# Scans of a gated DeltaNet block: projections beside them in parts of six products, and sums of squares with 128 columns of weights

## The chip, the cores and the metric

The kernel runs on one core of a Trainium2 chip. TensorE (PE) multiplies matrices into PSUM; VectorE (DVE), ScalarE (ACT) and GpSimd (POOL) do the elementwise work; SyncE (SP) issues most of the transfers. The metric is the time of one execution on the device in microseconds. A measurement is the median of several runs.

## What is computed

One block of a streaming encoder for a sequence of 1024 frames with 1024 channels in float32: half a SwiGLU layer, a mixing layer with two groups of heads (a gated spatial unit, and 4 heads of a gated delta rule), another half SwiGLU layer, and a last norm. The change touches only the delta rule. Cut to that:

```python
qkv = jax.nn.silu(causal_dwconv(qkv, dn_conv_w[l])).astype(jnp.float32)
q, k, v = jnp.split(qkv, 3, axis=-1)
q = l2norm(q.reshape(B, T, DN_HEADS, DN_HEAD_DIM))
k = l2norm(k.reshape(B, T, DN_HEADS, DN_HEAD_DIM))
...
sol = lax.linalg.triangular_solve(L + eye, rhs, left_side=True, lower=True, unit_diagonal=True)
u_c, w_c = sol[..., :Dv], sol[..., Dv:]
...
def step(S, inp):
    qd, kd, uc, wc, a, gl = inp
    v_new = uc - jnp.einsum('bhcd,bhde->bhce', wc, S)
    o = jnp.einsum('bhcd,bhde->bhce', qd, S) + jnp.einsum('bhij,bhje->bhie', a, v_new)
    S = S * jnp.exp(gl)[..., None, None] + jnp.einsum('bhcd,bhce->bhde', kd, v_new)
    return S, o
```

The recurrence over chunks (`step`) is the scan: each state `S` needs the one before it.

## The kernel before

The two SwiGLU layers take most of the time (`ffn`). Between them stands `middle`, where the delta rule is worked out in eight halves: 4 heads, each with two halves of the sequence of 512 frames. A half (class `Half`) holds four tiles of 128 frames and goes through these methods, all written as generators that yield between steps:

- `inverse`: five steps that put the inverse of a triangular matrix together from blocks of 32 and 64 rows, and its product with the keys. Each step is one group of small fp32 matmuls into a bank of `ps_a` (tag `ax`, two banks), and a copy or a subtraction out of it by ACT or DVE, into a buffer of the tag `rv` or into `Z` and `X`.
- `values`: two steps, transposes of the values (`VT`) and the product with `Z`, which give `u`.
- `queries`: two steps. The first squares the queries on ACT and sums them over channels by matmuls with a column of ones; the second makes the products of keys and queries.
- `scan`: for each of the four tiles two products with the state (`sc` and `sq`), a subtraction from `u` on DVE, a yield, the product `sd` that updates the state, and a yield. After the eighth yield comes a closing part: the product of `aT` and `u` (`ax<-u,aT` in the profile), its sum of squares on ACT, a norm, and multiplications with the gate `zt` and the norm on POOL. `zt` is loaded at the start of the scan into a buffer of the tag `rv`, of which there are two.

While a scan runs, its stage also issues the filler. `proj_steps` is one: the projection of one block of 128 channels of queries or values for the whole sequence. For each half of the sequence it makes 8 steps over the contraction, each of three products of 128x128 by 128x512 (`mm3`: high by high, high by low, low by high, since a float32 number is held as a rounded part of type fp32r and the rest), all into one bank of `ps_m`; then a copy to `pad` on ACT, a convolution of one multiplication (L1000) and three multiply-adds (L1002) on DVE, and a SiLU on ACT. Before the change it yields after each step of three products. The other filler is the preparation of later halves: nine small steps. In the stage of a first half `x` of head h these are `y.values`, `y.queries` and `nx.inverse` (`first`), in that of a second half `ny.inverse`, `nx.values` and `nx.queries` (`second`), where `y` is the second half of the same head and `nx`, `ny` are the halves of the next.

`weave(few, many, gaps)` mixes the two by hand: for each number n in `gaps` it issues n parts of the projection and then one small step. `stage(x, filler, rate)` runs the scan and pulls `rate` steps of the filler after each of its yields, and what is left once the scan's closing part is written. `beside` adds a step of the spatial unit's mixing (`mixing`) at the second, fifth and eighth small step. The framework orders instructions by this order of writing, but puts an instruction that is ready ahead of an earlier one that is not, by its own estimate of times, when it compiles; on the chip each engine runs its instructions in that order.

The stages that the change touches are five: the first halves of heads 0, 1 and 2 (projection of the next head's queries) and the second halves of heads 0 and 1 (projection of the values of the head after next). The second half of head 2 and both halves of head 3 have another filler, `token_steps` of the gated spatial unit (`u0`, `u1`), which is not changed.

Of the kernel before, what the change touches and what calls it, by code (L numbers as in the profile page):

```python
# [17 lines left out]
P = 128  # L18
T = 1024
D = 1024  # L20
KC = 8
NCH = 22
HEADS = 4
# [7 lines left out]
def block_kernel(ctx: ExitStack, tc, a, out):  # L31
# [579 lines left out]
    with ExitStack() as mid:  # L611
        ps_a, ps_s, ps_m = psums(mid, (2, 1, 3))
        tl = pool(mid, "tl")
        up = pool(mid, "up")
        lv = pool(mid, "lv")
        ep = pool(mid, "ep")
        ts = pool(mid, "ts")
        kp = pool(mid, "kp")
        wp = pool(mid, "wp")
        yblk = middle(tc, nc, a, locals())  # L620
# [190 lines left out]
def middle(tc, nc, a, L):  # L811
# [4 lines left out]
    bank, mm, mm3, split, rpow, rsqrt = L["bank"], L["mm"], L["mm3"], L["split"], L["rpow"], L["rsqrt"]  # L816
# [49 lines left out]
    def steps(name, ch, ev, **kw):  # L866
        w = a[f"w{name}"][ch]
        return token_steps([w[0], w[1]], 256, ev, hT, **kw)
# [6 lines left out]
    def sc(name, n=32):  # L875
        return ts.tile([P, n], F32, tag=name, name=name)
# [70 lines left out]
    def v4(t):  # L947
        return t.rearrange("p (t n) -> p t n", t=4)
# [4 lines left out]
    def tl(t):  # L953
        return slice(t * P, (t + 1) * P)

    def big(name, bufs=1):
        p = {"VT": lv, "rv": lv, "aT": lv, "u": up}.get(name, late)
        return p.tile([P, 512], F32, tag=name, name=name, bufs=bufs)
# [4 lines left out]
    def four(lf, rf, pp=(ps_a, "ax"), w=P):  # L963
        ps = bank(*pp)
        for t in range(4):
            mm(ps[:, t * w:t * w + w], lf(t), rf(t), start=True, stop=True)
        return ps
# [7 lines left out]
    def load_qkv(blk, behind=None):  # L975
        with tc.issue_after(behind.ins) if behind else nullcontext():
            return load_w(a["wqkv"][blk]).rearrange("p s (k n) -> p s k n", k=KC)

    def proj_conv(blk, dsts):
        for _ in proj_steps(blk, load_qkv(blk), dsts):  # L980
            pass

    def proj_steps(blk, w, dsts):
        prev = None
        for half in range(2):
            h = hT[half]
            ps = bank(ps_m, "mm")
            for k in range(KC):
                mm3(ps, w[:, 0, k], w[:, 1, k], h[k // 4][:, 0, k % 4], h[k // 4][:, 1, k % 4], k == 0, k == KC - 1)
                if k < KC - 1:  # L990
                    yield
            pad = ts.tile([P, 528], F32, tag="pad", name="pad", bufs=2)
            if half == 0:
                nc.gpsimd.memset(pad[:, 0:3], 0.0)
            else:
                nc.gpsimd.tensor_copy(pad[:, 0:3], prev[:, 512:515])
            prev = pad
            nc.scalar.copy(pad[:, 3:515], ps)
            acc = ep.tile([P, 512], F32, tag="acc", name="acc", bufs=2)
            nc.vector.tensor_scalar(acc, pad[:, 0:512], cw[:, blk, 0:1], None, op0=ALU.mult)  # L1000
            for j in range(1, 4):
                nc.vector.scalar_tensor_tensor(acc, pad[:, j:j + 512], cw[:, blk, j:j + 1], acc, op0=ALU.mult, op1=ALU.add)  # L1002
            d = dsts[half]
            nc.scalar.activation(d, acc if len(d.shape) == 2 else v4(acc), AF.Silu)
            yield

    def inv_norm(ss, scale, add, name):
        r = small("r" + name)
        nc.vector.tensor_scalar(r, ss, scale, add, op0=ALU.mult, op1=ALU.add)
        rpow(r, r, 4)  # L1010
        return r
# [48 lines left out]
    class Half:  # L1060
# [66 lines left out]
        def queries(self):  # L1127
            q = self.wq[:, :, P:256]
            aT = self.aT = big("aT", 2)
            nc.scalar.activation(v4(aT), q, AF.Square)  # L1130
            ssq = bank(ps_a, "ax")[:, :4]
            for t in range(4):
                for c in (0, 64):
                    mm(ssq[c:c + 64, t:t + 1], aT[:, t * P + c:t * P + c + 64], ones, start=True, stop=True)
            self.rq = inv_norm(ssq, P, P * EPS, "q")
            yield
            aps = four(lambda t: self.ks[:, 0, tl(t)], lambda t: q[:, t])
            nc.vector.tensor_tensor(aT, aps, EA[self.h][:, self.hf], op=ALU.mult)
            yield
# [39 lines left out]
    ones = sc("ones", 128)[:, 0:1]  # L1179
# [82 lines left out]
    def load_ya():  # L1262
        y = xp.tile([P, 2, 512], F32, tag="x", name="ya")
        t = 2 * len(ya)
        nc.sync.dma_start(y, sp["m"][t:t + 2].rearrange("t p n -> p t n"))
        ya.append(y)
# [24 lines left out]
    def values_of(h):  # L1291
        for x in H[h]:
            x.VT = big("VT", 4)
        return [x.VT for x in H[h]]

    def new_wq(x):
        x.wq = xp.tile([P, 4, 256], F32, tag="x", name="wq")

    def queries_of(h):
        return [x.wq[:, :, P:256] for x in H[h]]  # L1300


    def weave(few, many, gaps):
        for n in gaps:
            yield from islice(many, n)
            yield from islice(few, 1)
        yield from many
        yield from few
# [4 lines left out]
    def beside(steps):  # L1313
        for i, s in enumerate(steps):
            if i in (1, 4, 7):
                next(mixed, None)
            yield s

    def stage(x, filler, rate):
        due = 0.0  # L1320
        for _ in x.scan():
            due += rate
            while due >= 1:
                due -= 1
                next(filler, None)
        for _ in filler:
            pass
# [3 lines left out]
    with tc.issue_after(solved.ins):  # L1331
        wv, wq_ = load_qkv(9), load_qkv(1)
        together(proj_steps(8, w8, values_of(0)))
        together(proj_steps(0, w0, queries_of(0)))
# [4 lines left out]
    for h in range(HEADS):  # L1339
        x, y = H[h]  # L1340
        if h + 1 < HEADS:
            nx, ny = H[h + 1]
            nx.load()

            def first():
                yield from y.values()
                yield from y.queries()
                yield from nx.inverse()

            def queries():  # L1350
                for z in (nx, ny):
                    new_wq(z)
                yield from proj_steps(h + 1, wq_, queries_of(h + 1))

            def second():
                yield from ny.inverse()
                yield from nx.values()
                yield from nx.queries()

            if h + 2 < HEADS:  # L1360
                wv = load_qkv(10 + h, solved)
            else:
                u0 = steps("u", 0, ev_u0, part=2)
            stage(x, weave(beside(first()), queries(), (1,) + (2,) * 8), 2)
            ny.load()
            if h + 2 < HEADS:
                wq_ = load_qkv(h + 2)
                more = proj_steps(10 + h, wv, values_of(h + 2))
            else:
                more = islice(u0, 16)  # L1370
            stage(y, weave(beside(second()), more, (1, 1, 2, 2, 2, 2, 2, 2, 2)), 2)
        else:
            stage(x, weave(chain(y.values(), y.queries()), islice(u0, 8), (0, 1, 1, 1, 0)), 1.5)
            stage(y, u0, 1)
            u1 = steps("u", 1, ev_u1, part=2, tiles=(0, 4, 1, 5, 2, 6, 3, 7))
            for _ in range(4):
                load_ya()
            together(u1)
# [75 lines left out]
```

## Time and profile before

| what | value |
|---|---|
| three runs | 1818.42, 1818.73, 1819.32 us; median 1818.73 |
| the profiled execution | 1816.45 us |
| its span | 1814.4 us |
| mean granted clock of TensorE | 0.994 |
| instructions | 24818 |
| first scan's first product (`sc`) | at 867.6 us |
| last scan's closing product (`ax<-u,aT`) | at 1035.9 us |
| sums of squares (`ax<-ones,aT`) | 128 matmuls, 128 weight loads |

The page gives each engine's busy time, and the span in 40 slices, so that a stage can be found. The scans lie between about 867 and 1037 us, in slices 20 to 23. In rows of the timeline the first number is the start of a group of like instructions, the second the time from its first start to its last end, then the engine, the line of the kernel, the operation, what is written and read (`mm<-actT,wk` is a projection's product, `ax<-Z,L` and `ax<-rv,X` are steps of the inverse), the rows and columns of the weights (128*128), the shape that moves through them, and how many there are. A bracket at the end gives the idle time ahead of the group, and what ended it. All small matmuls have line L53, that of the helper `mm`, so groups are told apart by tiles.

### The profile page before, as it was taken

How to read it: one execution, taken by the hardware profiler on the slowest of the kernel's cores; microseconds unless marked ns; L12 is line 12 of the kernel's file. 1: busy time of each engine (PE TensorE's matmuls, PEld its weight loads, DVE VectorE, ACT ScalarE, POOL GpSimd, SP SyncE). 2: the span in 40 equal slices, each digit the busy share in tenths (PEclk: the TensorE clock that was granted, in tenths of full speed). 3: DMA queues.
4: the chain of work that ended last, by engine and by line, in shares of the span. 5: the costliest groups of instructions: out<-in, count | busy, mean ns of one | idle time of the engine just before them, and what ended most of it. 6: DMA issues, size and time to landing. Idle time of an engine off the chain costs nothing. (4 is left out here: it accounts for less than half of the span.)

```text
span 1814.4 us, 24818 instructions
## 1 busy us (share of the span) xinstructions
PE 1764.0 (97%) x9303; PEld 1491.6 (82%) x9303; DVE 1165.2 (64%) x1487; ACT 708.1 (39%) x1261; POOL 798.2 (44%) x656
## 2 busy tenths in 40 slices
PE   5999999999999999999999989899999999999997
PEld 4888888888888889897788978788888888888886
DVE  7867666555666575659675265777766767566545
ACT  6333333332443355633334553543333333244334
POOL 5757666565173021120232454667655656315002
PEclk9999999999999999999999999999999999999999
DMA  4354443544888545455332344335444444486744
GB/s 175 121 182 145 160 159 134 180 168 168 322 314 302 199 169 183 154 185 195 112 103 78 111 157 136 118 111 204 166 147 150 169 160 165 145 300 241 255 126 151
DMA packets 142730, 313.77 MB, mean 173 GB/s; under 512 B 28017, under 2 KB 42641, under 8 KB 142609
## 3 DMA queue, kind: packets, MB, share of 16 engines
q1 hardware_dynamic: 140112, 307.74, 49.0%
q10 hardware_dynamic: 2496, 4.44, 0.8%
q8 instruction: 73, 1.20, 0.3%
q14 instruction: 49, 0.39, 0.1%
HBM read 214.07 MB, written 98.06 MB: 172 GB/s over the span
## 5 line engine op out<-in xcount | busy, mean ns | idle before, releaser
L53 PE MATMUL mm<-unit 128*128 128x512 f32 x1056 | 243.0, 390 | 1.6 <-DVE unit L62 1.6
L53 PEld LDWEIGHTS mm<-unit 128*128 128x128 f32 x1056 | 197.7, 188 | 43.6 <-DVE unit L62 2.9
L62 DVE TENSOR_TENSOR gs<-s,gs 128x512 fp32r<-128x512 f32 x168 | 172.8, 1031 | 50.8 <-ACT gs L61 49.0
L61 ACT CAST gs<-s 128x512 fp32r<-128x512 f32 x168 | 104.0, 621 | 225.9 <-PE ax L53 104.6
L197 POOL TENSOR_TENSOR s<-graw 128x512 f32<-128x512 f32 x84 | 125.2, 1491 | 148.3 <-DMA graw<-in_f1gu_dram 98.2
L53 PE MATMUL ax<-T,gs 128*128 128x512 f32 x792 | 183.1, 389 | 0.0
L53 PE MATMUL ax<-unit 128*128 128x512 f32 x792 | 180.5, 389 | 0.0
L62 DVE TENSOR_TENSOR ga<-graw,ga 128x512 fp32r<-128x512 f32 x134 | 134.0, 1002 | 66.5 <-ACT ga L61 65.8
L53 PEld LDWEIGHTS ax<-T,gs 128*128 128x128 f32 x792 | 148.7, 188 | 30.8
L53 PEld LDWEIGHTS ax<-unit 128*128 128x128 f32 x792 | 148.7, 188 | 30.8
L62 DVE TENSOR_TENSOR unit<-left,unit 128x1024 fp32r<-128x1024 f32 x84 | 106.6, 1269 | 102.8 <-ACT unit L61 102.7
L53 PE MATMUL mm<-B,ga 128*128 128x512 f32 (+1 forms) x864 | 167.4, 347 | 3.6 <-ACT B L122 2.2
L53 PE MATMUL mm<-T,gs 128*128 128x512 f32 x720 | 166.4, 389 | 0.0
L53 PEld LDWEIGHTS mm<-B,ga 128*128 128x128 f32 x864 | 139.5, 193 | 23.4 <-ACT B L122 2.4
L53 PEld LDWEIGHTS mm<-T,gs 128*128 128x128 f32 x720 | 135.2, 188 | 28.0
L61 ACT CAST unit<-left 128x1024 fp32r<-128x1024 f32 x84 | 82.5, 982 | 191.8 <-PE ax L53 95.9
L53 PE MATMUL mm<-actT,wk 128*128 128x512 f32 x576 | 152.1, 406 | 0.0
L61 ACT CAST ga<-graw 128x512 fp32r<-128x512 f32 x134 | 82.9, 621 | 131.2 <-PE mm L53 49.1
L62 DVE TENSOR_TENSOR unit<-right,unit 128x1024 fp32r<-128x1024 f32 x84 | 111.3, 1325 | 27.0 <-ACT unit L61 27.0
L53 PE MATMUL ax<-B,ga 128*128 128x512 f32 x528 | 126.9, 389 | 0.0
L53 PE MATMUL mm<-wk,actT 128*128 128x256 f32 x960 | 122.1, 282 | 0.0
L53 PEld LDWEIGHTS mm<-actT,wk 128*128 128x128 f32 x576 | 104.1, 190 | 19.2
(250 smaller groups left out, 3006.2 us busy)
## 6 DMA issues: line engine op xcount, KB each, us to landing
left<-hq SPq DMA_DIRECT2D x70, 512.0 KB, 6.4
graw<-in_f1gu_dram SPq DMA_DIRECT2D x44, 512.0 KB, 5.8
wq<-t SPq DMA_DIRECT2D x44, 512.0 KB, 2.8
hq<-s SPq DMA_DIRECT2D x44, 512.0 KB, 3.2
graw<-in_f2gu_dram SPq DMA_DIRECT2D x44, 512.0 KB, 3.9
right<-wq SPq DMA_DIRECT2D x40, 512.0 KB, 4.7
wd<-in_f1wd_dram SPq DMA_DIRECT2D x22, 512.0 KB, 6.7
hq<-sg SPq DMA_DIRECT2D x22, 512.0 KB, 3.7
```

The source lines that it names most:

```text
L53: nc.tensor.matmul(*args, **kw)
L61: nc.scalar.copy(h, src)
L62: nc.vector.tensor_tensor(l, src, h, op=ALU.subtract)
L197: nc.gpsimd.tensor_tensor(f, u, v, op=op)
```

## The change

`proj_steps` gets a parameter `part`, the number of steps of three products between two yields. The five stages call it with 2, so that one part has six products and a projection eight parts instead of sixteen; the numbers in `gaps` follow, so that one part stands between two small steps throughout, where it was two parts in most places. In the stage of a first half the first small step now comes ahead of the first part. The projections before the first scan keep parts of three, and the stage of the second half of head 2 keeps its numbers.

In `queries` the sum of squares of each tile of 128 frames is one matmul with 128 columns of weights, where it was two with 64 columns that write to the lower and the upper 64 partitions.

```diff
-    def proj_steps(blk, w, dsts):
+    def proj_steps(blk, w, dsts, part=1):
...
-                if k < KC - 1:
+                if (k + 1) % part == 0 and k < KC - 1:
                     yield
...
             for t in range(4):
-                for c in (0, 64):
-                    mm(ssq[c:c + 64, t:t + 1], aT[:, t * P + c:t * P + c + 64], ones, start=True, stop=True)
+                mm(ssq[:, t:t + 1], aT[:, tl(t)], ones, start=True, stop=True)
...
-                yield from proj_steps(h + 1, wq_, queries_of(h + 1))
+                yield from proj_steps(h + 1, wq_, queries_of(h + 1), 2)
...
-            stage(x, weave(beside(first()), queries(), (1,) + (2,) * 8), 2)
+            stage(x, weave(beside(first()), queries(), (0,) + (1,) * 8), 2)
             ny.load()
             if h + 2 < HEADS:
                 wq_ = load_qkv(h + 2)
-                more = proj_steps(10 + h, wv, values_of(h + 2))
+                more = proj_steps(10 + h, wv, values_of(h + 2), 2)
             else:
                 more = islice(u0, 16)
-            stage(y, weave(beside(second()), more, (1, 1, 2, 2, 2, 2, 2, 2, 2)), 2)
+            gaps = (1, 1, 2, 2, 2, 2, 2, 2, 2) if h + 2 >= HEADS else (1,) * 8 + (0,)
+            stage(y, weave(beside(second()), more, gaps), 2)
```

## The prediction

> **What bounds the kernel now.** I read the page first: TensorE (PE) is busy for 97% of the span, and no other engine passes 64%. A busy share can hide gaps, so the second view is the table of windows over the scans that the change touches, and the third the waits of PE alone over 860 to 993 us.
>
> ```profile
> PE 1764.0 (97%) x9303; PEld 1491.6 (82%) x9303; DVE 1165.2 (64%) x1487; ACT 708.1 (39%) x1261; POOL 798.2 (44%) x656
> ```
>
> ```profile
> 880.00:900.00 20.00, 19.34 (x181) 15.70 (x181) 10.92 (x23) 9.00 (x24) 6.05 (x8) 1.00 0.32 93
> 900.00:920.00 20.00, 20.00 (x159) 16.59 (x159) 14.90 (x34) 6.79 (x18) 5.10 (x8) 1.00 0.39 115
> 920.00:940.00 20.00, 19.60 (x161) 16.37 (x159) 16.74 (x35) 7.32 (x19) 6.46 (x9) 1.00 0.37 125
> ```
>
> ```profile
> PE sd L53 <- DVE u L1155: 1.1, 2, 0.7
> ```
>
> In a window the first figure after the length is PE's busy time: 19.34, 20.00 and 19.60 of 20 us, at a granted clock of 1.00. PE waited in 133 us only twice, 1.1 us in all, both times for VectorE's (DVE's) update of `u`. So the five stages that change (the scans of both halves of heads 0 and 1 and of the first half of head 2) are bound by the number of PE instructions and by what stands between two kinds of them. Moving a product inside a stage changes no count. Only three things can move the time: what the sums of squares cost PE, what PE waits for, and how often groups of unlike matmuls are cut apart.
>
> The fourth view is PE's timeline, because starts there show what a group really occupies (the next group's start minus its own); durations of pipelined matmuls overlap.
>
> ```profile
> 839.64 9.00 PE L53 MATMUL mm<-actT,wk 128*128 128x512 f32 x39
> 848.58 0.59 PE L53 MATMUL ax<-Z,L 32*32 32x32 f32 x16
> ...
> 873.30 1.05 PE L53 MATMUL ax<-rv,Z 128*128 128x128 f32 x8
> 874.29 0.63 PE L53 MATMUL ax<-ones,aT 128*64 128x1 f32 x16
> 874.85 0.98 PE L53 MATMUL mm<-actT,wk 128*128 128x512 f32 x3
> 875.66 1.05 PE L53 MATMUL ax<-wq,ks 128*128 128x128 f32 x8
> 876.55 0.60 PE L972 MATMUL ax<-ident,VT 128*128 128x128 f32 x4
> ...
> 958.11 1.06 PE L53 MATMUL ax<-Z,ks 128*128 128x128 f32 x8
> 958.92 0.94 PE L53 MATMUL mm<-actT,wk 128*128 128x512 f32 x3
> 959.70 0.38 PE L53 MATMUL sd<-u,ks 128*128 128x128 f32 x2
> ```
>
> A projection's product occupies (848.58 - 839.64) / 39 = 0.229 us, a part of six 1.37 us, a part of three 0.69. Eight fp32 matmuls with 128 columns of weights occupy 876.55 - 875.66 = 0.89 us, 0.111 each.
>
> **The sums of squares.** One call of `queries()` issues 8 products, recorded as 16 matmuls (two for each) with 64 columns of weights and one moving column; the change makes them 8 with 128 columns. What the 16 occupy, with the change of shape before and after them, comes from two like stretches: eight matmuls, the sums, three products, up to the next group take 875.66 - 873.30 = 2.36 us; the same without sums takes 959.70 - 958.11 = 1.59 us. The sums cost 0.77 us of PE. The merged 8 aren't in the trace. The nearest row has the same eight loads of 128 columns and more moving columns: 0.89 us. One moving column can't make them dearer as long as the load sets the pace, so I take 0.89: **+0.12 us a call, +1.0 us over 8 calls**. Below: if they ran at the pace of the present sums, 0.56 / 16 = 0.035 us each, with no change of shape around them, a call would be 0.28 us, 0.49 less, 3.9 us less over 8 calls. Above: if each load stood bare and a matmul's 0.035 came on top of 0.111, a call would be 1.17 us, 0.40 more, 3.2 us over 8. Nobody on PE's path waits for these sums: `rq` is used only in the scan's closing step, more than a microsecond later.
>
> Two rules of the Trainium skill meet here. "TensorEngine Tiling (Array Packing)", section Key Properties, says that a change of tiling mode drains TensorE, which speaks for the change; the trace agrees, as the sums' 0.77 us is 0.21 more than their own 0.56. "TensorE: Matmul & The Clock Gate", section LDWEIGHTS, gives a load as columns / 1.2 ns, whatever the rows, which speaks against it: an estimate from it is 8 x 107 ns = 0.85 us, +0.7 us over 8 calls. The trace's 0.111 agrees.
>
> **The parts of six.** One projection has 2 halves x 8 steps x 3 = 48 products, before and after; 16 parts of 3 become 8 of 6. In a stage the scan yields 8 times and pulls two steps of filler each time: 16. The old filler has 9 small steps (f1 to f9: inverse, values, queries) and 16 parts, so 9 of its 25 steps lay behind the scan; the new one has 9 + 8 = 17, and only f9 is left. Between two small steps lie six products, as in most places before. That the issued order follows the written one is seen in the trace, with small moves: the planner puts a ready matmul ahead of one that isn't.
>
> ```profile
> 878.36 0.38 PE L53 MATMUL ax<-rv,Z 128*128 128x128 f32 x2
> 878.58 0.39 PE L53 MATMUL sc<-S,wq 128*128 128x128 f32 x2
> 878.81 0.39 PE L53 MATMUL sq<-S,wq 128*128 128x128 f32 x2
> 879.03 0.83 PE L53 MATMUL ax<-rv,Z 128*128 128x128 f32 x6
> ...
> 898.84 0.49 PE L53 MATMUL sd<-u,ks 128*128 128x128 f32 x2 [0.66 <-DVE u L1155]
> ...
> 903.45 0.33 PE L53 MATMUL ax<-Z,L 64*64 64x64 f32 x2
> 903.71 0.49 PE L53 MATMUL sd<-u,ks 128*128 128x128 f32 x2
> 904.13 0.56 PE L53 MATMUL ax<-Z,L 64*64 64x64 f32 x6
> 904.62 0.73 PE L53 MATMUL mm<-actT,wk 128*128 128x512 f32 x2
> ...
> 907.02 0.49 PE L53 MATMUL sd<-u,ks 128*128 128x128 f32 x2
> 907.27 1.64 PE L53 MATMUL mm<-actT,wk 128*128 128x512 f32 x6
> ...
> 923.65 0.49 PE L53 MATMUL sd<-u,ks 128*128 128x128 f32 x2 [0.40 <-DVE u L1155]
> ...
> 940.98 0.68 PE L53 MATMUL ax<-Z,L 64*64 64x64 f32 x8
> 941.59 0.96 PE L53 MATMUL mm<-actT,wk 128*128 128x512 f32 x3
> ...
> 952.15 0.44 PE L53 MATMUL ax<-Z,L 64*64 64x64 f32 x4
> ```
>
> Cuts: a 64x64 group cut by `sd` takes 904.62 - 903.45 = 1.17 us, where the whole group is 0.61 (941.59 - 940.98) and `sd` 0.25 (907.27 - 907.02): 0.31 us a cut. Two of the five stages have one (903.45 and 952.15 us). Larger parts change who is ready when, so they may vanish or stay; I take one of two, **-0.3 us**, bounds -0.6 and +0.3.
>
> Waits: the two stalls, 0.66 and 0.40 us, are the price of a projection that ends just ahead of a scan.
>
> ```profile
> 922.31 1.08 DVE L1000 TENSOR_SCALAR acc<-pad,cw 128x512 f32<-128x512 f32 x1
> 923.32 0.27 DVE L1155 TENSOR_TENSOR u<-u,sc 128x128 f32<-128x128 f32 x1
> 923.51 0.74 DVE L1002 SCALAR_TENSOR_TENSOR acc<-pad,cw,acc 128x512 f32<-128x512 f32 x1
> ```
>
> The convolution that follows each half of a projection (one such L1000, then three L1002 of 0.74) stands on DVE's queue ahead of the scan's `u`, and `sd` on PE waits for `u`. Afterwards the last part still ends just ahead of the next scan, with only the scan's closing product and f9 between (0.89 us each by the group of eight). The convolutions also come at the fourth part, in the middle of the scan. What hides them there is the next part of six, 1.37 us, and a small step; if that cover were gone, each would cost up to the 0.66 us of the worst stall. So stalls move but needn't end: I take **0**, with bounds of -1.1 (both gone) and +2.2 (0.66 in each of the five stages, less 1.1).
>
> No DMA is added. The loads of the next half (`load`) and of the weights stay where they were written, between two stages; the steps that move issue none, but for the mixing steps beside them (a load and a store of `vs`, on SP's queue). The one row of PE's waits names no DMA, so a delay on SP's queue would have to pass a whole stage's work before PE saw it; I take 0.
>
> **Sum.** +1.0 - 0.3 + 0 = +0.7 us. The profiled execution took 1816.45 us (span 1814.4), 0.13% under the median of 1818.73, so it would become 1817.15; for the timed runs I forecast 1818.73 + 0.7 = **1819.4 us**. Its own bounds: the small terms alone give -0.6 - 1.1 and +0.3 + 2.2 around +1.0, so 1818.0 to 1822.2.
>
> **Rivals.** *Slower: the shared buffer.* The tag `rv` has two buffers, for the scan's gate `zt`, the values' product and the inverse's intermediates. `zt` is held until GpSimd (POOL) has multiplied it in at the end of the scan.
>
> ```profile
> 886.43 1.05 PE L53 MATMUL ax<-u,aT 128*128 128x128 f32 x8
> ...
> 912.13 1.06 PE L53 MATMUL ax<-u,aT 128*128 128x128 f32 x8
> ...
> 921.50 0.39 PE L53 MATMUL sc<-S,wq 128*128 128x128 f32 x2
> ```
>
> On POOL's timeline that multiplication is L1173:
>
> ```profile
> 890.53 1.27 POOL L1173 TENSOR_TENSOR oh<-oh,rv 128x512 f32<-128x512 f32 x1 [3.26 <-ACT ax L1170]
> ...
> 917.20 1.27 POOL L1173 TENSOR_TENSOR oh<-oh,rv 128x512 f32<-128x512 f32 x1 [1.24 <-ACT ax L1170]
> ```
>
> From the closing product to the end of that multiplication pass 890.53 + 1.27 - 886.43 = 5.4 us and 917.20 + 1.27 - 912.13 = 6.3 us. Today 9.4 us (921.50 - 912.13) lie between closing product and next scan, filled by the nine steps left over. Afterwards the next scan begins about 1.8 us behind it and takes the second buffer for its own `zt`; its first small step needs a third. In a first-half stage f2 is due about 3.4 us behind the closing product (1.8, the two products of the scan 0.45, f1, a part) and can't start before 5.4: 2 to 3 us late. In a second-half stage f2 is due at about 5 us and comes at 6 to 7: 1 to 2 late. If the planner leaves f2 where it is written, PE stands for 2 x 2.5 + 3 x 1.5 = 9.5 us: 1828.9. If it puts one part of 1.37 us ahead each time, some 2.7 us remain, 1822.1, and with two nothing does. It decides from the place of f2 in PE's queue. For it: the buffers are counted in the code, and the cover shrinks from 9.4 to 1.8 us. Against it: the cut groups show that the planner moves ready matmuls ahead, and parts are always ready. I give it 0.16, most likely at 1824 to 1829.
>
> *Faster: the merged sums run at the pace of the old ones.* Then -3.9 - 0.3 = -4.2 and 1814.5; with the stalls gone too, 1813.4. For it: a matmul with one moving column streams almost nothing. Against it: eight groups of 128-column loads all stand at 0.111 each. The Trainium skill, "TensorEngine Tiling (Array Packing)", section Instruction Overhead, would give this: about 60 cycles a matmul for any free size up to 60, with nothing for the load. The trace's 0.035 for 64 columns is near that rule and 0.111 for 128 columns far from it. Together with savings that I don't see I give it 0.15.
>
> *The change does not do what it says*: the planner, free to reorder, issues nearly the old order, and only the sums remain: +1.0, 1819.7. I give it 0.03; by time it isn't to be told from the forecast.
>
> **How the numbers follow.** Forecast 0.66, order unchanged 0.03, shared buffer 0.16, fast sums 0.15. 0.2% is 3.6 us, about what a measurement of this kernel can tell from no change: faster is below 1815.1, slower above 1822.4. Faster 0.15, within 0.69, slower 0.16. The range takes in the fast sums with both cuts gone (3.9 + 0.6 below 1818.73 is 1814.2) and goes most of the way to bare loads with a cut and a stall in every stage (3.2 + 0.3 + 2.2 above it is 1824.4): 1814.2 to 1823.5. It leaves out the shared buffer in the order written.
>
> **What would show it.** The sums: 64 matmuls `ones` of 128x128 weights instead of 128, and the group of eight followed by the next after 0.89 us (0.28 by the rival). The order: products in groups of six between small steps, and the next scan's `sc` 1 to 3 us behind a closing product instead of 9.4. Waits of PE in the five stages: about 1 us, for `u`; if the buffer decides, several microseconds, before `ax<-rv,Z` and `ax<-rv,X`, released by ACT or DVE writing `rv`. I am wrong if the time from the first to the last scan changes by over 3 us with PE's waits unchanged, or if a stage outside the five moves.

## The result, and the profile after

| four runs each | median, us | range | ratio to before |
|---|---|---|---|
| before | 1819.03 | 1818.42 to 1820.22 | |
| after | 1829.59 | 1826.20 to 1831.27 | 1.0058 (95%: 1.0046 to 1.0069) |

The changed kernel is slower by about 10.6 us, 0.58%. The forecast was 1819.4 us, and its range ended at 1823.5: it was wrong. What came instead is the mechanism of the rival of the shared buffer; its time, 1824 to 1829, is close too, but for other reasons than its price (see below). The profiled execution of after took 1829.83 us (span 1827.9, mean granted clock 0.993, 24690 instructions: 64 matmuls and 64 weight loads fewer).

The page of after starts with the busy times. PE's share is the same 97%, so the page alone doesn't show what happened.

```profile
PE 1767.6 (97%) x9239; PEld 1497.7 (82%) x9239; DVE 1168.2 (64%) x1487; ACT 704.3 (39%) x1259; POOL 801.2 (44%) x656
```

The table of windows over the same three stretches as in the prediction: length, then busy time and count of PE, PEld, DVE, ACT and POOL, the granted clock, the DMA share, GB/s.

```profile
880.00:900.00 20.00, 20.00 (x173) 17.87 (x173) 11.10 (x24) 5.20 (x12) 3.09 (x6) 1.00 0.38 113
900.00:920.00 20.00, 18.80 (x146) 15.27 (x145) 15.12 (x33) 8.04 (x23) 7.36 (x9) 1.00 0.22 66
920.00:940.00 20.00, 18.58 (x131) 16.57 (x129) 12.44 (x26) 7.22 (x19) 8.31 (x10) 0.91 0.45 138
...
930.00:934.00 4.00, 2.58 (x21) 2.13 (x19) 1.04 (x3) 0.95 (x2) 3.58 (x5) 0.98 0.59 181
934.00:937.00 3.00, 3.00 (x12) 2.71 (x13) 1.47 (x5) 0.00 (x0) 1.01 (x1) 0.50 0.14 22
```

Two things are new: PE is idle for 1.2 and 1.4 us in the second and third row, and in the third the clock falls to 0.91. The finer rows show where: 4.00 - 2.58 = 1.42 us of idle time, and behind it a spell at half clock (0.50).

The waits of PE in after, over 860 to 1010 us (engine, what it writes, the line, the releaser; us in all, times, the longest):

```profile
PE ax L53 <- ACT rv L1089: 2.9, 3, 1.4
PE ax L53 <- DVE rv L1120: 2.8, 2, 1.4
PE ax L53 <- DVE Z L1096: 1.3, 1, 1.3
PE sc L53 <- DVE S L1161: 0.9, 2, 0.5
```

The third is in the preparation ahead of the scans (at 861 us). The others are new: five waits for a write to `rv`, by the inverse (L1089) or by the values (L1120), and two for the state. Each of the five changed stages is followed by just one wait for `rv`. PE's timeline of after shows the rows that count at two boundaries, and the waits at the other three:

```profile
876.89 1.05 PE L53 MATMUL ax<-rv,Z 128*128 128x128 f32 x8
...
879.37 1.05 PE L53 MATMUL ax<-wq,ks 128*128 128x128 f32 x8
...
898.18 1.05 PE L53 MATMUL ax<-u,aT 128*128 128x128 f32 x8
...
899.97 0.39 PE L53 MATMUL sc<-S,wq 128*128 128x128 f32 x2
...
900.33 1.62 PE L53 MATMUL mm<-actT,wk 128*128 128x512 f32 x6
...
902.64 1.87 PE L53 MATMUL mm<-actT,wk 128*128 128x512 f32 x7
904.97 0.49 PE L53 MATMUL sc<-S,wq 128*128 128x128 f32 x2 [0.46 <-DVE S L1161]
906.20 0.71 PE L53 MATMUL ax<-rv,X 32*32 32x32 f32 x16 [0.75 <-ACT rv L1089]
...
923.75 1.16 PE L53 MATMUL ax<-u,aT 128*128 128x128 f32 x8
924.75 0.39 PE L53 MATMUL sc<-S,wq 128*128 128x128 f32 x2
...
926.01 2.09 PE L53 MATMUL mm<-actT,wk 128*128 128x512 f32 x8
...
928.51 1.17 PE L53 MATMUL mm<-actT,wk 128*128 128x512 f32 x4
...
929.88 0.94 PE L53 MATMUL mm<-actT,wk 128*128 128x512 f32 x3
932.24 1.13 PE L53 MATMUL ax<-rv,Z 128*128 128x128 f32 x8 [1.42 <-DVE rv L1120]
...
957.92 0.49 PE L53 MATMUL sc<-S,wq 128*128 128x128 f32 x2 [0.40 <-DVE S L1161]
959.15 0.71 PE L53 MATMUL ax<-rv,X 32*32 32x32 f32 x16 [0.74 <-ACT rv L1089]
...
985.17 1.13 PE L53 MATMUL ax<-rv,Z 128*128 128x128 f32 x8 [1.40 <-DVE rv L1120]
...
1008.78 0.71 PE L53 MATMUL ax<-rv,X 32*32 32x32 f32 x16 [1.40 <-ACT rv L1089]
```

The next scan's `sc` starts 1.8 us (899.97 - 898.18) and 1.0 us (924.75 - 923.75) behind the closing product. The waits at the five boundaries add up to 0.46 + 0.75 + 1.42 + 0.40 + 0.74 + 1.40 + 1.40 = 6.6 us. Before, PE waited 1.1 us.

The profile names ACT and DVE as releasers, but neither was late by its own work. The rows of those engines and of POOL in after, at the first two boundaries (in after, lines behind the sums have numbers lower by one: L1172 multiplies the gate in, L1164 multiplies the gate with the norm's weights):

```profile
902.23 0.62 ACT L1163 ACTIVATE rv<-rv 128x512 f32<-128x512 f32 x1
...
905.89 0.53 ACT L1089 COPY rv<-ax 32x128 f32<-32x128 f32 x2 [1.75 <-POOL oh L1172]
...
931.40 0.69 DVE L1120 TENSOR_TENSOR rv<-ax,brk 128x512 f32<-128x512 f32 x1 [1.25 <-POOL oh L1172]
...
902.92 1.71 POOL L1164 TENSOR_TENSOR rv<-rv,dn_norm 128x512 f32<-128x512 f32 x1 [12.61 <-PE sd L53]
904.60 1.26 POOL L1172 TENSOR_TENSOR oh<-oh,rv 128x512 f32<-128x512 f32 x1
...
928.84 1.29 POOL L1164 TENSOR_TENSOR rv<-rv,dn_norm 128x512 f32<-128x512 f32 x1 [5.40 <-DVE wk L62]
930.09 1.28 POOL L1172 TENSOR_TENSOR oh<-oh,rv 128x512 f32<-128x512 f32 x1
```

The copy to `rv` (L1089) and the multiplication to `rv` (L1120) sat idle until L1172 had read the ended scan's `zt` for the last time. That is the buffer. From closing product to its release pass 904.60 + 1.26 - 898.18 = 7.7 us and 930.09 + 1.28 - 923.75 = 7.6 us, where the prediction had 5.4 to 6.3. L1164 ahead of it belongs to the *next* scan: its gate was loaded early and its SiLU (L1163) and its multiplication went ahead of the old scan's L1172.

To add the parts up I use the stretch from the first `sc` to the last matmul of the last `ax<-u,aT`: 867.61 to 1036.70 us before, 871.20 to 1048.23 after, so 169.09 and 177.03 us, 7.9 more. Of these, 6.6 - 1.1 = 5.5 are waits, about 1.7 the spell at half clock (3.4 us long), +1.0 the sums and -0.6 the cut groups, which are gone: 7.6 us. The rest of the span, outside the stretch, is 1645.3 us before and 1650.9 after. Of these 5.6 us, 3.6 lie ahead of the first `sc` (871.20 - 867.61), where PE, DVE, ACT and POOL run the same instructions in the same order in both kernels; so that part isn't work that the change added. In eleven profiles (these two, and all experiments below but the two with repeated sums) the rest lies anywhere from 1645.3 to 1651.8. The profiled run of before is at the lower end, so the stretch tells more than the span. The medians differ by 10.6 us, 2.7 more than the stretch; no trace explains these 2.7.

### The profile page after: what moved, and what is told of

Same layout as the page of the kernel before. It is cut to its first block, busy times and chain, and to the rows that moved or that the text cites. A ratio compares the mean times of both kernels' runs of the same rounds, so it can differ in the third digit from the quotient of the medians.

```text
span 1827.9 us, 24690 instructions
## 1 busy us (share of the span) xinstructions
PE 1767.6 (97%) x9239; PEld 1497.7 (82%) x9239; DVE 1168.2 (64%) x1487; ACT 704.3 (39%) x1259; POOL 801.2 (44%) x656
## 5 line engine op out<-in xcount | busy, mean ns | idle before, releaser
L62 DVE TENSOR_TENSOR gs<-s,gs 128x512 fp32r<-128x512 f32 x168 | 172.6, 1029 | 53.1 <-ACT gs L61 51.2
L53 PE MATMUL mm<-actT,wk 128*128 128x512 f32 x576 | 147.2, 401 | 0.0
```

The source lines that it names most:

```text
L53: nc.tensor.matmul(*args, **kw)
L62: nc.vector.tensor_tensor(l, src, h, op=ALU.subtract)
```

## The experiments

Two theories were open. **The buffer:** what counts is how soon the next scan begins behind the closing part, against how long `zt` holds one of the two buffers of `rv`. **The parts of six** (or the sums): larger parts, whatever the boundary, leave dependent work late, or the new sums cost more than their starts show. Times are medians, ratios are to before with 95% intervals, "stretch" is that of the profiled run.

### A third buffer

```diff
-            Pm = big("rv", 2)
+            Pm = big("rv", 3)
...
-            zt = big("rv", 2)
+            zt = big("rv", 3)
...
-    ones = sc("ones", 128)[:, 0:1]
+    ones = sc("ones", 8)[:, 0:1]
```

The changed kernel with three buffers of the tag in all four places where one is taken; the column of ones sits in a smaller tile to make room.

> The changed kernel with three buffers for the tag rv instead of two (the column of ones takes a smaller tile to make room). Theory (the gate zt of the scan that ends and that of the next hold both buffers, so the next small step waits): the waits of PE for rv (6.6 us in the trace of the changed kernel, 906 to 1009 us) are gone, and with them the spell of half clock at 934 us; what is left over the kernel before are the sums, +1.0, and small waits: 1819.5 to 1822. Rival (six products and one convolution less cover, whatever the buffers): waits stay within 2 us of 6.6 and the time stays at 1826 to 1831.

Measured: 1821.99 us, ratio 1.0018 (1.0010 to 1.0027); stretch 169.84 us. The waits of PE over 860 to 1010 us, in this kernel, are one row:

```profile
PE sc L53 <- DVE S L1161: 0.2, 1, 0.2
```

Every wait for `rv` is gone with the parts, the order and the sums of the changed kernel kept; no spell of half clock is left in the scans, and 7.2 of the 7.9 us in the stretch are back. What stays in the stretch, 0.75 us, is about the size of the sums' term, looked at below.

### Only the sums

The kernel before with the merged sums and nothing else.

```diff
-                for c in (0, 64):
-                    mm(ssq[c:c + 64, t:t + 1], aT[:, t * P + c:t * P + c + 64], ones, start=True, stop=True)
+                mm(ssq[:, t:t + 1], aT[:, tl(t)], ones, start=True, stop=True)
```

> The kernel before with the merged sums of squares alone. By the starts in the timeline (0.77 us for 16 matmuls with their changes of shape, 0.89 for 8 loads of 128 columns) PE has 0.12 us more a call: +1.0 us, 1819 to 1821. Rival 1 (the merged sums run at 0.035 us each): 1814 to 1816. Rival 2 (they shift the planner's order and are part of the loss): above 1822.

Measured: 1821.01 us, ratio 1.0009 (1.0000 to 1.0017); stretch 169.45, 0.4 more than before. The median is at the upper end of what was expected. The sums can't be the cause of 10 us.

### A slower pull

The changed kernel, but its five stages pull three parts for every two yields of the scan, not four, so that more of the filler is left for the time behind the scan.

```diff
-            stage(x, weave(beside(first()), queries(), (0,) + (1,) * 8), 2)
+            stage(x, weave(beside(first()), queries(), (0,) + (1,) * 8), 1.5)
...
-            stage(y, weave(beside(second()), more, gaps), 2)
+            stage(y, weave(beside(second()), more, gaps), 2 if h + 2 >= HEADS else 1.5)
```

> The changed kernel, with 1.5 steps of filler for each yield of the scan instead of 2 in the five stages: 12 of the 17 steps lie in the scan and 5 behind it, so some 6 us of work lie between a closing product and the next scan. Theory (the distance between the scans decides, since zt is held 5 to 8 us): waits for rv under 2 us, 1819 to 1823. Rival (parts of six are too coarse a cover): as the changed kernel, 1826 to 1831.

Measured: 1824.10 us, ratio 1.0025 (1.0016 to 1.0034); stretch 170.87. PE's timeline of this kernel at the first boundary shows the distance:

```profile
890.89 1.05 PE L53 MATMUL ax<-u,aT 128*128 128x128 f32 x8
...
899.41 0.39 PE L53 MATMUL sc<-S,wq 128*128 128x128 f32 x2
```

The `sc` follows 8.5 us behind, and PE's waits over 860 to 1010 us are:

```profile
PE sd L53 <- DVE u L1154: 0.7, 1, 0.7
PE ax L53 <- DVE Z L1096: 0.6, 1, 0.6
```

Parts of six with two buffers don't wait for `rv` once the distance is back. The wait for `u` is of the kind that the kernel before had. The stretch gets back 6.2 of its 7.9 us, the median 5.5 of 10.6, which leaves it 1.1 us above the range expected; what lies between was not traced further.

### Parts of three, pulled as far

The converse: the kernel before with its parts of three and its old sums, but three parts a yield in the five stages, so that its filler is used up within the scan too.

```diff
-            stage(x, weave(beside(first()), queries(), (1,) + (2,) * 8), 2)
+            stage(x, weave(beside(first()), queries(), (1,) + (2,) * 8), 3)
...
-            stage(y, weave(beside(second()), more, (1, 1, 2, 2, 2, 2, 2, 2, 2)), 2)
+            stage(y, weave(beside(second()), more, (1, 1, 2, 2, 2, 2, 2, 2, 2)), 2 if h + 2 >= HEADS else 3)
```

> The kernel before (parts of three, old sums), with 3 steps of filler for each yield instead of 2 in the same five stages: 24 of 25 steps lie in the scan, as in the changed kernel. Theory (distance between the scans): the same waits for rv at the same places, 4 to 8 us, 1823 to 1830. Rival (size of the parts): no such waits, 1818 to 1821.

Measured: 1830.01 us, ratio 1.0064 (1.0049 to 1.0079); stretch 178.89. Its waits of PE over 860 to 1010 us:

```profile
PE ax L53 <- ACT rv L1089: 2.9, 3, 1.4
PE sc L53 <- DVE S L1162: 1.4, 4, 0.5
PE ax L53 <- DVE rv L1120: 0.4, 2, 0.2
```

Nothing of the change is in this kernel but the tight boundary, and it is as slow as the changed one, with the same releasers. So the size of the parts is not the cause. That the times are so close is in part chance: its waits are less than those of after (4.7 us, of which 3.3 are for `rv`, where 4 to 8 were expected), but its clock is worse. The windows of this kernel:

```profile
900.00:904.00 4.00, 2.80 (x28) 1.73 (x28) 1.93 (x5) 1.18 (x4) 3.84 (x5) 1.00 0.76 261
904.00:908.00 4.00, 4.00 (x29) 3.33 (x28) 2.08 (x6) 0.37 (x1) 0.40 (x1) 0.57 0.12 27
```

PE is idle for 4.00 - 2.80 = 1.2 us (waits of 0.45 and 0.75), and behind that a spell at half clock begins that lasts 6.8 us. A second one of 6.8 us begins at 1007 us, behind a wait of 1.40. Half of the 13.7 us is lost, 6.8.

### A later gate

The changed kernel with the same two buffers, but `zt` is taken and loaded at the third tile of the scan, not at its start.

```diff
-            zt = big("rv", 2)
-            nc.sync.dma_start(v4(zt), sp["z"][hf * 4:hf * 4 + 4, :, h * P:(h + 1) * P].rearrange("t p n -> p t n"))
...
             for t in range(4):
+                if t == 2:
+                    zt = big("rv", 2)
+                    nc.sync.dma_start(v4(zt), sp["z"][hf * 4:hf * 4 + 4, :, h * P:(h + 1) * P].rearrange("t p n -> p t n"))
```

> The changed kernel, two buffers of rv as before, but each scan takes its buffer for the gate zt, and loads it, at its third tile instead of at its start. Theory (the next scan's zt takes the second buffer while the old one is still held): with the second buffer free at the start of a scan, the small steps find it, and the 6.6 us of waits for rv fall under 2 us: 1820 to 1823, as with three buffers. Rival (the old zt alone is what is waited for, or the work on POOL and ACT is late for another reason): waits stay above 4 us, 1826 to 1831.

Measured: 1821.51 us, ratio 1.0021 (1.0012 to 1.0030); stretch 172.48. PE's timeline of this kernel:

```profile
895.25 1.05 PE L53 MATMUL ax<-u,aT 128*128 128x128 f32 x8
...
897.04 0.39 PE L53 MATMUL sc<-S,wq 128*128 128x128 f32 x2
...
901.28 0.59 PE L53 MATMUL ax<-rv,X 32*32 32x32 f32 x16
...
1026.37 0.49 PE L53 MATMUL sq<-S,wq 128*128 128x128 f32 x2 [2.44 <-ACT oh L1157]
```

The boundary is as tight as in after (1.8 us), and `ax<-rv,X` has no bracket: it waits for nothing. ACT and POOL of this kernel show which buffer was free (lines behind the moved load have numbers higher by one than in after):

```profile
899.84 0.52 ACT L1089 COPY rv<-ax 32x128 f32<-32x128 f32 x2
...
900.01 1.70 POOL L1173 TENSOR_TENSOR oh<-oh,rv 128x512 f32<-128x512 f32 x1 [12.62 <-ACT ax L1170]
```

The copy to `rv` was done at 899.84 + 0.52 = 900.36, before POOL had read the old `zt` to its end (900.01 + 1.70 = 901.71), so it had the second buffer. So the second lifetime matters, not the number of buffers as such: the next scan's gate held the second buffer while it wasn't needed.

The last row of PE is a wait of 2.4 us in the last head, outside the five stages, with a spell of half clock behind it (3.4 us); together they make up for the 2.6 us by which the stretch is longer than with a third buffer. This is a price of the later load: ACT stood until the gate had arrived, and the scaling of `sq` (L1157) that PE waited for came behind it.

```profile
1024.14 1.28 ACT L1164 ACT_TABLE_LOAD   x1 [5.42 <-DMA rv<-spz]
```

The same edit on the kernel before, as a control:

> The kernel before with the late gate alone. In it 9.4 us lie between the closing product and the next scan, so the buffers do not bind: within 1 us of the kernel before, 1818 to 1820. Rival (the late load of the gate costs by itself, at the closing part of each scan): above 1822, which would also burden the two kernels above.

Measured: 1819.61 us, ratio 1.0009 (1.0000 to 1.0018); stretch 169.83. The later gate gains nothing where the boundary isn't tight; the wait of `sq` for ACT in the last head is there too, 1.0 us.

### The old sums in three of these kernels

The diff is that of "only the sums", the other way round, made to the changed kernel, to the one with the later gate, and to the one with three buffers.

> The changed kernel with the sums of 64 columns of weights as before. If the sums are the small term that the starts show (0.12 us a call), the time falls by 1 to 2 us, to 1827 to 1829, and the waits for rv stay at 5 to 8 us. Rival (the merged sums and the new order make each other worse): below 1825.

Measured: 1826.87 us, ratio 1.0043 (1.0030 to 1.0055); stretch 177.27, in which a spell of half clock of 6.8 us is twice as long as that of after. The waits for `rv` are the same 2.9 and 2.8 us, though not one sum of the new form is left.

> Parts of six with the late gate and the old sums. Theory: the sums' 1 us less than with the late gate alone, 1819 to 1821, at best as the kernel before; parts of six have nothing to gain over parts of three, since PE waited only 1.1 us in the scans before. Rival (parts of six would gain once the buffers are out of the way): under 1817.

Measured: 1818.40 us, ratio 0.9996 (0.9988 to 1.0005); stretch 168.36, the shortest of all, 0.7 less than before. That is what parts of six give once the buffer is out of the way: the two cuts of 0.3 us, and no difference in time that can be told from none (the interval takes in 1).

> Parts of six with three buffers of rv and the old sums. Theory: as with the late gate and the old sums, within 1.5 us of the kernel before, 1817.5 to 1820; with the merged sums it was 1822.0, so this also gives the sums' price a third time (1 us by the starts in the timeline, 2 to 3 us by the medians so far). Rival (the merged sums cost nothing in this order): 1821 to 1823.

Measured: 1821.02 us, ratio 1.0011 (1.0002 to 1.0020); stretch 168.85, 1.0 us under that of the third buffer with merged sums. The stretch is as expected, the median isn't: it lies above 1817.5 to 1820 and just inside the range of the rival, by which the merged sums cost nothing here. By itself this median doesn't decide between the two.

Against the medians of the kernel before that were taken beside them (1818.49 for the first two, 1819.18 for the third) these are +8.4, -0.1 and +1.8 us; with the merged sums it was +10.6, +3.0 and +3.1 us (against 1819.03, 1818.49 and 1818.86). The merged sums thus cost 2.2, 3.1 and 1.3 us in these pairs, and 2.1 (0 to 3.1 by the interval) on the kernel before. By starts they cost 1.0 us, and the stretches of the third pair agree with that. The medians lean to more, and that stays open.

### The sums five times

To measure the disputed matmul by itself, each sum is issued five times, once in the merged form and once in the old, on the kernel before.

```diff
-            for t in range(4):
+            for t in list(range(4)) * 5:
```

> The kernel before with the merged sums, each issued five times over (same results, 4 x 8 matmuls more a call, 8 calls). At 0.89 us for eight, 4 x 0.89 x 8 = 28.5 us more than with the merged sums once: 1848 to 1851. If one moving column made them cheaper than the load of 128 columns, at 0.035 each, it would be 9 us: 1830.

> The kernel before with the old sums of 64 columns, each issued five times over (4 x 16 matmuls more a call, 8 calls; the change of shape is paid once). At 0.46 to 0.56 us for sixteen, 15 to 18 us more than the kernel before: 1834 to 1837. If the two halves of the columns did not overlap, 0.89 us for sixteen and 1847.

Measured: merged 1872.56 us, ratio 1.0289 (1.0273 to 1.0304); old 1840.18 us, ratio 1.0120 (1.0106 to 1.0134). Both are above what was expected, 1848 to 1851 and 1834 to 1837. PE's timeline, merged:

```profile
930.80 4.52 PE L53 MATMUL ax<-ones,aT 128*128 128x1 f32 x40
935.18 0.49 PE L53 MATMUL mm<-actT,wk 128*128 128x512 f32 x1
```

and old:

```profile
924.30 2.50 PE L53 MATMUL ax<-ones,aT 128*64 128x1 f32 x80
926.73 2.76 PE L53 MATMUL ax<-vs,gmc 128*128 128x128 f32 x16
```

Merged: 4.38 / 40 = 0.1095 us each, 0.88 a call of eight. Old: 2.43 / 80 = 0.030 us each, 0.49 for sixteen, with little of the change of shape, which is spread over eighty. So the rival "fast sums" is false, and the prediction's price was right. The 32 further merged matmuls of a call would be 32 x 0.1095 x 8 = 28.0 us in all; the kernel lost 51.2 against the merged sums issued once (53.4 and 2.1 us over the kernel before, 1819.18 and 1818.86 in these two comparisons). The windows of the merged run say where the rest went:

```profile
930.00:935.00 5.00, 5.00 (x44) 4.83 (x42) 0.75 (x1) 1.82 (x6) 1.33 (x2) 1.00 0.27 69
935.00:938.00 3.00, 3.00 (x17) 2.95 (x18) 0.93 (x3) 0.00 (x0) 2.25 (x4) 0.61 0.00 0
...
949.00:959.00 10.00, 10.00 (x44) 9.42 (x44) 3.09 (x10) 0.37 (x1) 2.55 (x3) 0.52 0.11 43
```

PE is busy without a gap, and yet the clock falls to half: right behind the sums in the second row, and for nearly all of the third, where a spell lasts 10.2 us. Such spells, one at each of the eight calls, take about 51 us of this kernel's stretch, half of which, 25.6 us, is lost: 28.0 + 25.6 = 53.6, close to the 51.2 measured. The old form loses less: 64 x 0.0304 x 8 = 15.6 us directly and 13.6 us of spells, 6.8 lost, 22.4 in all against 21.0 measured (1840.18 - 1819.18).

## Why the prediction was wrong

- **What bounds the kernel:** right that PE bounds it. But "only three things can move the time" left out a fourth, the granted clock, which took about 1.7 us in after and 6.8 with parts of three pulled as far.
- **The sums, +0.12 us a call:** right. In after, eight matmuls, the sums, three products, up to the next group take 879.37 - 876.89 = 2.48 us, where 2.36 stood before. The medians suggest more than 1.0 us for eight calls. Spells of half clock as with the sums issued five times aren't the reason in these traces: with the merged sums once and no long wait (only the sums, the third buffer, the slower pull) the stretch has none. It stays open.
- **The cuts, -0.3:** the mechanism was right and the size too small. Both cuts are gone: -0.6.
- **The order** came as forecast: parts of six between small steps, and the next scan 1.0 to 1.8 us behind a closing product. "The change does not do what it says" is false.
- **The waits are the step that failed:** "So stalls move but needn't end: I take 0", with +2.2 as the upper bound. That term looked at the convolution ahead of `u` alone. It had left the wait for `rv` to a rival, and the range left that rival out. The wait for `u` did vanish from the five stages; the wait for `rv` took its place, 6.6 us with those for the state, 5.5 net, and about 1.7 for the clock behind it.
- **The rival's mechanism** was right in each step: the tag, its two holders, the release by POOL, and the place of the wait. Its price was 9.5 us for no help by the planner and 2.7 for one part ahead; the waits were 5.5 net. That 1829.59 is so close to the 1828.9 of the full price is luck: the clock's 1.7 and the 2.7 that no trace explains make up for the 4.0 of waits that didn't come.
- **Two things moved that price.** The planner helped, but unevenly. As the code writes it, twelve products stand between the next scan's first `sc` and its second small step in a second-half stage; thirteen were issued (six at 900.33, seven at 902.64). In a first-half stage six are written and fifteen were issued (926.01, 928.51, 929.88). And the buffer came free 7.6 to 7.7 us behind the closing product, not 5.4 to 6.3. In the old order POOL was done with the old scan's L1173 (917.20 + 1.27 = 918.5) before the next scan's first `sc` (921.50). In the new one the next scan's gate is ready early and goes ahead of it, 1.3 to 1.7 us on POOL and 0.6 on ACT between the squares. With the later gate, where none goes ahead at that boundary, the same release comes at 900.01 + 1.70 - 895.25 = 6.5 us. So the release was read off the old order, and the change that made the boundary tight also delayed it.
- **The chance:** 0.16 was too low. The argument against the rival, that ready parts are moved ahead, was true but had been given no size at the boundary: by the prediction's own numbers a buffer free at 5.4 to 6.3 us, against work due at 3.4 and 5, needed up to two parts in front to vanish, and the quoted rows showed groups cut, not two parts moved.

The theory of the buffer is shown from four sides: with a buffer more, with a later allocation, and with a wider boundary the waits go, and with a tight boundary and the old parts they come. Spells of half clock within the stretch go with the waits: where PE never stands there for longer than 1.0 us (seven of the eleven profiles) there is none, in the other four there are one or two. No version here beats the kernel before; parts of six with the later gate and the old sums equal it.

## What to carry to other kernels

Steps left over behind a loop can be the cover under which the loop's last holders give back their buffers: before filler is drawn into a loop, list for each tag what is held across the boundary, when its last reader ends, and what the next loop takes at its start. Work that release time out in the new order, since the next loop's early work may go ahead of the last reader. Where the boundary has to be tight, take long-lived buffers as late as their use allows, but leave time for what is loaded into them: with the later gate ACT stood 5.42 us for the load in the last head.

## What the hardware showed that was not expected

**Half clock after short waits.** In after 1.42 us of idle PE, with eight one-column sums right behind, was followed by 3.4 us at half clock; with parts of three pulled as far, waits of 0.45 and 0.75 us, with no sums near, were followed by 6.8 us. The like waits of 1.40 us at 985.17 and 1008.78 in after weren't. The spells are 3.4, 6.8 or 10.2 us long, multiples of one length. "TensorE: Matmul & The Clock Gate" in the Trainium skill, section Part 1 on the clock gate, says that the gate watches a window of about 3.4 us that runs freely, and that an idle window of it throttles. The length and the chance in it agree with these runs; if it means a window idle as a whole, that does not, since PE was idle for only 1.2 to 1.4 us.

**Half clock with a busy PE.** Forty one-column matmuls with 128 columns of weights in a row (4.4 us) were followed by half clock though PE showed no gap. In the profile PE was loading weights for nearly all of it (4.83 of 5.00 us) and streamed one column per load. What the gate counts can't be told from these runs.

**Weight loads of 64 columns** into the two column halves in turn take 0.030 us each, 128 columns 0.1095: 3.6 times as long for twice the columns. So the form with twice the instructions was the cheaper one, 0.49 against 0.88 us for eight products, and the change of shape around it took 0.77 - 0.49 = 0.28 us of that back.
